# A recurrent mixer's chunk stage: undecayed keys kept and summed for the bonus, end decays straight from PSUM, a later copy, second buffers, another order of pieces

## The chip, the cores and the metric

The kernel runs on one core of one Trainium2 chip. The metric is the device time of one execution in microseconds, the median of several runs. The two layers of the network are written out one after the other in one program, so what one stage gains or loses counts twice.

## The reference, cut to what matters

Each of two layers runs three groups of heads side by side: windowed attention (A), attention with rotary positions (B), and a bidirectional RWKV-7 recurrence (C, six heads of 64). The change touches C alone. Cut to that, for one direction `d`:

```python
decay = exp(-exp(wlog))                                # from tanh(xw) @ w_up[d]
a  = sigmoid(a0[d] + xa @ a_up[d])
kt = heads(k * (1.0 + (a - 1.0) * k_a))                # the undecayed key
for each token:                                        # forward for d = 0, backward for d = 1
    sa = S @ (-kk)
    S  = S * decay + outer(sa, kk * a) + outer(v, kt)
    y  = S @ r
y_sum += y
bonus += sum(r * kt * r_k) * v                         # over both directions
```

The bonus needs, for each token, the sum of `kt` over the two directions.

## The kernel before, in words

C is computed in chunks of 64 tokens. Five tiles of 128 tokens make five groups, each a pair of a forward and a backward tile: (0,3), (1,2), (4,4), (2,1), (3,0). Each tile so comes up twice, once for each direction. For a group g there are four kinds of work:

- `front(g)`: small matmuls give `tanh` of the decay and of `a` (L1074 to L1085), a matmul with a triangle sums the decays (L1092, bank pc), and ACT makes from it the decay `Pe` (L1097) and its inverse `iP` (L1098). `Pe` and `iP` have one buffer each. ACT makes `1 + (a-1) k_a` (L1100), DVE the gradient factor b (L1105, L1113) and the key (L1106, then L1114 with `iP`), POOL and DVE the products `W` (L1111, L1112). POOL copies the end decay PC out of `Pe` (L1117), and ACT copies b into the third part of the tile `BK` (L1115). When a tile comes up the second time, POOL adds `tanh(a)` of that direction into a tile `THS` (L1102). Then PE forms chunk products `GB` (L1130), of which ACT and DVE read the banks (L1132, L1133, L1137), transposes (L1163) follow with ACT copies (L1167).
- `relay(g)`: the 16x16 blocks of a triangular system go through DRAM (L1150, L1174), POOL inverts them on the tile `V` in 15 steps of two operations (L1180, L1182), copies the transpose (L1184), and SP writes both back (L1186). `V` is one tile; the next relay clears it with a memset (L1175).
- `solve(g)`: SP reads the inverses back (L1194), PE widens them to the 64x64 inverse in four rounds (L1202), each ended by a DVE operation (L1213, L1223).
- `step(g, d, i)`: the recurrence over the chunks (L1246 to L1300).

`bonus(t)` forms `z = c2 * THS + c1x2` (ACT, L1337, three times a tile), `z * k` (POOL, L1338), `z * r * r_k` (DVE, L1340) and a matmul.

All of these are generators cut into pieces, and a string of letters, `WEAVE`, says which stream yields its next piece: a, b, g, j, m are front 0 to 4; d, f, i, l, n are solve 0 to 4; e, h, k, o, p are the steps of groups 0 to 4; c builds v and the states; v and w are bonuses and outputs; q to u are out-projection work. "g6" below is the sixth piece of g. The string thus is the order of TensorE (PE); the queues of ACT, DVE, POOL and SP are ordered by a scheduler from the same program. The stage stands at about 303 to 589 us in layer 0 and 1351 to 1633 us in layer 1.

Of the kernel before, what the change touches and what calls it, by code (L numbers as in the profile page):

```python
# [38 lines left out]
WEAVE = ("aqqaaqaqaqqqqqaqqaqqqqaqaqqqqqqqqqcabbabbcbccccdbdccbddcbdccbbbdgdcegddeegggfgfgeegffgefeeeefeeggfjjjhjjhffhjihhhhjhhhjhjhjmmijikiiiimiimmkkmkkmlmkmllkkklkkvlkrlnlnllmnmnnonnnnnrvnonovovvowowvprrroooppwwwssrwpsspssswpwsswppppuwppwstwuxtttttwtttxtyttuuytutxyutuuuuuuuuu",  # L39
         "aqqaaqaqaqqqqqaqqaqqqqaqaqqqqqqqqqcabbabbcbccccdbdccbddcbdccbbbdgdcegddeegggfgfgeegffgefeeeefeeggfjjjhjjhffhjihhhhjhhhjhjhjmmijikiiiimiimmkkmkkmlmkmllkkklkkvlkrlnlnllmnmnnonnnnnrvnonovovvowowvprrroooppwwwssrwpsspssswpwsswppppuwppwstwuxtttttwtttxtyttuuytutxyutuuuuuuuuu")  # L40
# [82 lines left out]
def places(mem):  # L123
# [3 lines left out]
                ("c1x2", 6), ("kkhc", 6), ("sink", 8), ("nsink", 8))  # L127
# [3 lines left out]
    b = mem.lay("F", a, ("THS", 3 * TOK), *many("PC", range(6), 6), ("Pe0", 400), *many("Xf", (0, 1), 384), *many("St", (0, 1), 192), *many("SC", (0, 1), 192))  # L131
# [5 lines left out]
    mem.lay("F", y, ("V", 256), ("iP0", 384))  # L137
# [28 lines left out]
    mem.lay("M", 0, *many("W", (0, 1), 1536), *many("GB", (0, 1), 768), *many("TK", (2, 3), 768), *many("E", (0, 1), 384), *many("Xi", (0, 1), 384))  # L166
# [46 lines left out]
def trunk_kernel(ctx, tc, I, O, dbg=None, depth=DEPTH):  # L213
    nc = tc.nc
# [77 lines left out]
    c1x2 = mem.get("c1x2", [6])  # L292
# [3 lines left out]
    nc.vector.tensor_scalar(out=c1x2, in0=kac, scalar1=-1.0, scalar2=2.0, op0=ALU.mult, op1=ALU.add)  # L296
# [270 lines left out]
    for l in range(depth):  # L567
        if True:
# [499 lines left out]
            def front(g):  # L1068
                for d in range(2):
# [404 lines left out]
            with tc.manual_schedule(engines={PE}):  # L1474
                tiles5 = lambda ts, k0, k1: chain(*[out_part(t, k0, k1) for t in ts])
                streams = [front(0), front(1), chain(calls(*[(build_v, c) for c in range(10)]), calls((states, 0), (states, 1))), solve(0)]
                for g in range(5):
# [3 lines left out]
                    if g < 3:  # L1481
# [162 lines left out]
```

## Time and profile before

| what | before |
|---|---|
| time, median of 3 runs | 2146.09 us (2143.97 to 2146.56) |
| the profiled execution's own time | 2146.71 us |
| its span in the trace | 2144.9 us |
| PE busy | 1957.5 us (91%) |
| DVE, ACT, POOL busy | 1185.5, 815.7, 356.9 us |
| mean granted PE clock | 0.951 |
| the chunk stage of layer 0 | 286 us, PE busy 234.62 us of it |

The own time is the span and 1.8 us around it. PE's share over the whole says that most stages are bound by PE; the chunk stage is where PE has gaps and a lower granted clock, and it is the stage that the change touches.

### The profile page before, as it was taken

To read this page: it belongs to the slowest core of one execution; us is meant where nothing else is said; L and a number is where in the kernel's file an instruction comes from. 1 tells how busy PE (TensorE), PEld (TensorE's weight loads), DVE (VectorE), ACT (ScalarE), POOL (GpSimd) and SP (SyncE) were. 2 spreads that over 40 slices of the span, in tenths; PEclk is the share of its full clock that TensorE was granted. 3 is DMA by queue.
4 is the path that set the end of the run, shared out by engine and by line. 5 is a ranking of instruction groups with operands and counts; after the bars stand their busy time and mean duration, and the time that the engine had idled before them with its cause. 6 is when DMAs were issued, how large, how long until landed. Compare 5 with 4: busy or idle time off the path is not lost. (4 is left out here: it accounts for less than half of the span.)

```text
span 2144.9 us, 40077 instructions
## 1 busy us (share of the span) xinstructions
PE 1957.5 (91%) x16508; PEld 1713.4 (80%) x16508; DVE 1185.5 (55%) x2319; ACT 815.7 (38%) x1787; POOL 356.9 (17%) x644
## 2 busy tenths in 40 slices
PE   7999998778989999999989989968799999999997
PEld 2766787666769979989977878856677998998996
DVE  3657564565876636556267784356677522232324
ACT  4456543342562222212245673343335522221221
POOL 0210012562022112111022000254411000000002
PEclk8999999788999999999999999977899999999999
DMA  8264302224335445354232002022242322222221
GB/s 289 73 204 152 89 24 39 33 44 83 113 103 172 138 128 148 116 150 118 85 101 78 2 2 69 14 45 39 51 125 84 99 79 74 74 74 74 79 69 49
DMA packets 262334, 192.15 MB, mean 90 GB/s; under 512 B 107316, under 2 KB 225038, under 8 KB 262152
## 3 DMA queue, kind: packets, MB, share of 16 engines
q1 hardware_dynamic: 242672, 140.13, 23.6%
q0 software_dynamic: 8800, 29.17, 4.7%
q10 hardware_dynamic: 10680, 20.31, 2.8%
q8 instruction: 129, 2.11, 0.4%
q14 instruction: 53, 0.43, 0.1%
HBM read 173.48 MB, written 16.08 MB: 88 GB/s over the span
## 5 line engine op out<-in xcount | busy, mean ns | idle before, releaser
L549 PE MATMUL psb<-H,B 128*128 128x320 f32 x2112 | 319.8, 311 | 3.6 <-DVE H L541 2.8
L549 PEld LDWEIGHTS psb<-H,B 128*128 128x128 f32 x2112 | 313.5, 189 | 8.5 <-DVE H L541 3.5
L549 PE MATMUL psb<-H,A 128*128 128x320 f32 x2016 | 306.0, 311 | 0.0
L549 PEld LDWEIGHTS psb<-H,A 128*128 128x128 f32 x2016 | 298.4, 189 | 2.2 <-issue 1.2
L367 DVE TENSOR_TENSOR A<-F,A 128x1024 fp32r<-128x1024 f32 (+1 forms) x78 | 93.2, 1195 | 139.2 <-ACT A L366 139.2
L367 DVE TENSOR_TENSOR B<-F,B 128x1024 fp32r<-128x1024 f32 (+1 forms) x78 | 94.1, 1207 | 133.9 <-ACT B L366 133.9
L499 POOL TENSOR_TENSOR r<-v,F 128x1 f32<-128x1 f32 (+1 forms) x50 | 41.1, 824 | 715.6 <-DVE v L497 704.7
L366 ACT CAST A<-F 128x1024 fp32r<-128x1024 f32 (+1 forms) x78 | 80.0, 1026 | 206.8 <-PE psb L549 94.8
L366 ACT CAST B<-F 128x1024 fp32r<-128x1024 f32 x80 | 83.0, 1038 | 180.7 <-PE psb L549 111.1
L549 PE MATMUL psb<-H,C 128*128 128x320 f32 x864 | 130.6, 309 | 0.0
L549 PEld LDWEIGHTS psb<-H,C 128*128 128x128 f32 x864 | 127.8, 188 | 0.2
L400 POOL DMA_DIRECT2D F<-in_w_mod x96 | 71.9, 750 | 326.4 <-DVE F L406 217.5
L408 DVE SCALAR_TENSOR_TENSOR F<-F 128x512 f32<-128x512 f32 x168 | 114.6, 745 | 19.7 <-DMA F<-in_w_mod 14.5
L1572 DVE TENSOR_TENSOR F<-F,psb 128x320 f32<-128x320 f32 x88 | 42.8, 487 | 121.9 <-PE psb L549 121.9
L559 PE MATMUL psb<-A,M 128*128 128x512 f32 x370 | 96.7, 390 | 0.0
L367 DVE TENSOR_TENSOR C<-F,C 128x1024 fp32r<-128x1024 f32 (+1 forms) x34 | 40.5, 1192 | 79.1 <-ACT C L366 79.1
L559 PEld LDWEIGHTS psb<-A,M 128*128 128x128 f32 x370 | 69.2, 188 | 15.4 <-issue 1.0
L559 PE MATMUL psb<-B,M 128*128 128x512 f32 x310 | 77.6, 390 | 0.0
L858 DVE TENSOR_REDUCE mx<-psb 128x1 f32<-128x640 f32 (+3 forms) x100 | 64.6, 648 | 19.6 <-PE psb L840 15.9
L1566 ACT ACTIVATE F<-psb 128x320 f32<-128x320 f32 x88 | 38.2, 435 | 97.2 <-PE psb L549 95.3
L645 PE MATMUL psb<-B,H 128*128 128x512 f32 x240 | 63.6, 410 | 9.0 <-DVE B L367 5.9
L366 ACT CAST C<-F 128x1024 fp32r<-128x1024 f32 (+1 forms) x34 | 34.8, 1022 | 92.1 <-PE psb L559 46.6
(423 smaller groups left out, 3901.4 us busy)
## 6 DMA issues: line engine op xcount, KB each, us to landing
F<-in_w_gu SPq DMA_DIRECT2D x88, 512.0 KB
F<-in_w_mod POOLq DMA_DIRECT2D x96, 256.0 KB, 3.5
F<-in_w_in SPq DMA_DIRECT2D x40, 512.0 KB
F<-in_w_down SPq DMA_DIRECT2D x40, 512.0 KB
F<-in_w_mod SPq DMA_DIRECT2D x26, 512.0 KB
M<-in_w_mod SPq DMA_DIRECT2D x12, 512.0 KB
H<-in_w_mod SPq DMA_DIRECT2D x10, 512.0 KB
F<-in_w_out SPq DMA_DIRECT2D x40, 128.0 KB
```

The costliest lines, as they stand in the source:

```text
L366: nc.scalar.copy(out=hi[:, :n], in_=rawt[:, :n])
L367: (eng or nc.vector).tensor_tensor(out=lo[:, :n], in0=rawt[:, :n], in1=hi[:, :n], op=ALU.subtract)
L400: dma.dma_start(out=rv, in_=w[:, :, c0:c0 + n])
L408: nc.vector.scalar_tensor_tensor(out=ac[s][:, cc], in0=r[:, cc], scalar=sT[:, k, s:s + 1], in1=ac[s][:, cc], op0=ALU.mult, op1=ALU.add)
L499: nc.gpsimd.tensor_tensor(out=r, in0=v, in1=mhalf.to_broadcast(shape), op=ALU.pow)
L549: nc.tensor.matmul(out=ps2[hf][:, :HALF], lhsT=w[:, k, :], rhs=a[k][:, tk], start=(k == 0 and q == 0), stop=(k == KD - 1 and q == 2))
L559: nc.tensor.matmul(out=ps5[t], lhsT=a[k][:, tk], rhs=w[:, kk, :], start=(first and kk == 0 and q == 0), stop=(last and kk == nk - 1 and q ...
L645: nc.tensor.matmul(out=ps, lhsT=a[k0 + kk][:, tk], rhs=w[:, kk, :], start=(i == 0 and q == 0), stop=(i == n - 1 and q == 2))
L858: nc.vector.reduce_max(out=mx, in_=self.S, axis=AX.XY if self.nb == 5 else AX.X)
L1566: nc.scalar.activation(out=sgt[:, HALF * hf:HALF * hf + HALF], in_=pg[hf][:, :HALF], func=AF.Silu)
L1572: nc.vector.tensor_tensor(out=sgt[:, tk], in0=sgt[:, tk], in1=pu[hf][:, :HALF], op=ALU.mult)
```

## The change

- The tile `THS` gives way to `KS`. At a tile's first visit the undecayed key is made in `KS`; at its second in the third part of `BK`, and DVE adds it into `KS`. The POOL addition at L1102 is gone (5 a layer), and so are the bonus's three ACT operations (15 a layer) and its POOL product (5 a layer); five DVE additions a layer are new.
- The end decays PC are made by ACT with an exponential of 128x6 straight from the bank pc (10 a layer) instead of copied by POOL from `Pe`.
- The ACT copy of b moves from the end of the front's second and fourth piece to behind the two `GB` pieces.
- `V` and `iP` get a second buffer each. `Pe` stays at one.
- `WEAVE` is another string of the same letters.

```diff
-WEAVE = ("aqqaaqaqaqqqqqaqqaqqqqaqaqqqqqqqqqcabbabbcbccccdbdccbddcbdccbbbdgdcegddeegggfgfgeegffgefeeeefeeggfjjjhjjhffhjihhhhjhhhjhjhjmmijikiiiimiimmkkmkkmlmkmllkkklkkvlkrlnlnllmnmnnonnnnnrvn...
+WEAVE = ("aqqaaqaqaqqqqqaqqaqqqqaqaqqqqqqqqqcabcabbbdbccccbdcccbdbcdcbbdddgdgdfcebgeegggfgeegffgefeeefeeegjgjhjfjjhffhhjhhhjhhhijhjhjmmijkimiiiiimikmkkmkmlmkmllkkkkllvkklrnlllnmnnmnonnnnnrvn...
...
-            iPR = mem.ring("iP", 1, [3, 2, 64])
+            iPR = mem.ring("iP", 2, [3, 2, 64])
...
-            U, V = (mem.get(nm, [16, 16], parts=96) for nm in ("U", "V"))
+            U, VR = mem.get("U", [16, 16], parts=96), mem.ring("V", 2, [16, 16], parts=96)
...
-                    tha = BK[:, :, :, 2] if t in seen else ch(THS[:, :, tk])
+                    tha = BK[:, :, :, 2]
...
                     nc.scalar.activation(out=iP, in_=pcv[:, :, :, i0:i0 + 64], func=AF.Exp, scale=CDEC)
+                    PC = un["PC"] = PCS.take()
+                    jc = 64 if d == 0 else 0
+                    nc.scalar.activation(out=PC, in_=pcv[:, :, :, jc:jc + 1], func=AF.Exp, scale=-CDEC)
+                    first, KSt = t not in seen, ch(KS[:, :, tk])
+                    kin = KSt if first else BK[:, :, :, 1]
                     for pr in range(3):
-                        nc.scalar.activation(out=BK[:, pr, :, 1], in_=tha[:, pr], func=AF.Identity, scale=col1(c2, pr), bias=col1(c1, pr))
-                    if t in seen:
-                        nc.gpsimd.tensor_tensor(out=ch(THS[:, :, tk]), in0=ch(THS[:, :, tk]), in1=tha, op=ALU.add)
+                        nc.scalar.activation(out=kin[:, pr], in_=tha[:, pr], func=AF.Identity, scale=col1(c2, pr), bias=col1(c1, pr))
...
-                    nc.vector.tensor_tensor(out=BK[:, :, :, 1], in0=BK[:, :, :, 1], in1=ch(ckT[:, :, tk]), op=ALU.mult)
+                    kd = KSt if first else BK[:, :, :, 2]
+                    nc.vector.tensor_tensor(out=kd, in0=kin, in1=ch(ckT[:, :, tk]), op=ALU.mult)
...
-                    nc.vector.tensor_tensor(out=BK[:, :, :, 1], in0=BK[:, :, :, 1], in1=iP, op=ALU.mult)
-                    nc.scalar.copy(out=BK[:, :, :, 2], in_=BK[:, :, :, 0])
-                    jc = 64 if d == 0 else 0
-                    nc.gpsimd.tensor_copy(out=PC, in_=Pe[:, :, :, jc:jc + 1])
+                    nc.vector.tensor_tensor(out=BK[:, :, :, 1], in0=kd, in1=iP, op=ALU.mult)
+                    if not first:
+                        nc.vector.tensor_tensor(out=KSt, in0=KSt, in1=kd, op=ALU.add)
...
                         yield
+                    nc.scalar.copy(out=BK[:, :, :, 2], in_=BK[:, :, :, 0])
                     src = GB
...
-                z = THS[:, :, tk]
-                for pr in range(3):
-                    nc.scalar.activation(out=z[:, pr], in_=z[:, pr], func=AF.Identity, scale=col1(c2, pr), bias=col1(c1x2, pr))
-                nc.gpsimd.tensor_tensor(out=z, in0=z, in1=ckT[:, :, tk], op=ALU.mult)
+                z = KS[:, :, tk]
```

Three places of the queues. First ACT around the second half of front 2 in layer 0, before: L1079 to L1098 make tanh, `Pe` and `iP`; L1337 is the first bonus; L1132 reads the `GB` banks of g5 and g6.

```order
L1079 ACTIVATE F<-psb 128x384
L1085 ACTIVATE F<-psb,F 128x2x64 x3
L1100 ACTIVATE F<-F 128x2x64
L1097 ACTIVATE F<-psb 128x390
L1098 ACTIVATE F<-psb 128x384
L1100 ACTIVATE F<-F 128x2x64 x2
L1337 ACTIVATE F<-F 128x128 x2
L1115 COPY F<-F 128x6x64
L1132 COPY A<-psb 128x3x64
L1337 ACTIVATE F<-F 128x128
L1132 COPY A<-psb 128x3x64
```

The same place after the change (L1078, L1084, L1096, L1097, L1105 and L1134 are L1079, L1085, L1097, L1098, L1100 and L1132 of before; L1100 is the new exponential, L1141 the copy of b):

```order
L1078 ACTIVATE F<-psb 128x384
L1084 ACTIVATE F<-psb,F 128x2x64 x3
L1255 COPY H<-psb 128x192
L1105 ACTIVATE F<-F 128x2x64
L1262 COPY H<-psb 64x192
L1105 ACTIVATE F<-F 128x2x64
L1096 ACTIVATE F<-psb 128x390
L1097 ACTIVATE M<-psb 128x384
L1100 ACTIVATE F<-psb 128x6
L1105 ACTIVATE F<-F 128x2x64
L1134 COPY A<-psb 128x3x64
L1141 COPY F<-F 128x6x64
```

The bonus's L1337 no longer stands ahead of the copies L1134 that empty the `GB` banks; the copy of b stands behind the first of them.

POOL at the end of relay 1 in layer 0, before: L1184 is the relay's last operation, L1175 and L1176 clear `V` for relay 2, L1111 are the `W` products of front 2.

```order
L1184 COPY N<-F 96x256
L1175 MEMSET F 96x256
L1176 MEMSET F 96x16
L1102 TENSOR_TENSOR F<-F 128x3x128
L1111 TENSOR_TENSOR A<-F 64x6x64 x2
L1117 COPY F<-F 128x6
L1338 TENSOR_TENSOR F<-F 128x3x128
L1287 TENSOR_TENSOR F<-H,F 128x192 x3
```

After it (L1188 and L1179 are L1184 and L1175 of before, L1114 is L1111; relay 1 now works on the buffer in zone M):

```order
L1186 TENSOR_TENSOR M<-M,N 96x15
L1188 COPY N<-M 96x256
L1179 MEMSET M 96x256
L1180 MEMSET M 96x16
L1114 TENSOR_TENSOR A<-F 64x6x64 x2
L1291 TENSOR_TENSOR F<-H,F 128x192 x3
```

The additions and the copy are gone, and the memset still stands between the relay's end and the second pair of `W` products, now on the tile that the relay has just left.

DVE around the first rounds of solve 2 (L1213, L1223) and front 4 in layer 0, before; L1340 is the bonus:

```order
L1112 TENSOR_TENSOR H<-C,F 64x6x64
L1113 SCALAR_TENSOR_TENSOR F<-F 128x6x64
L1114 TENSOR_TENSOR F<-F 128x6x64
L1213 TENSOR_TENSOR M<-psb,F 128x384
L1340 SCALAR_TENSOR_TENSOR F<-F 128x128 x3
L1223 TENSOR_TENSOR F<-psb,N 128x384 x2
L1223 TENSOR_TENSOR M<-psb,N 128x384 x2
```

After it (L1217 and L1227 are L1213 and L1223, L1119 is the new addition, L1341 the bonus, L1079 the first DVE operation of front 4's second half):

```order
L1117 TENSOR_TENSOR F<-F 128x6x64
L1119 TENSOR_TENSOR F<-F 128x3x128
L1217 TENSOR_TENSOR M<-psb,F 128x384
L1341 SCALAR_TENSOR_TENSOR F<-F 128x128 x2
L1079 TENSOR_SCALAR F<-F 128x384
L1341 SCALAR_TENSOR_TENSOR F<-F 128x128
L1227 TENSOR_TENSOR F<-psb,N 128x384
```

The bonus's three operations still stand ahead of the second round's L1227, but they need no POOL product any more, and an addition stands ahead of L1217.

## Rows read from the trace of the kernel before

**Rows 1.** The page, engines: busy us, share of the span, instructions.

```profile
PE 1957.5 (91%) x16508; PEld 1713.4 (80%) x16508; DVE 1185.5 (55%) x2319; ACT 815.7 (38%) x1787; POOL 356.9 (17%) x644
```

**Rows 2.** Windows over the stage: length, busy of each engine, PEclk, DMA share, GB/s.

```profile
371.30:403.30 32.00, 18.09 (x272) 14.40 (x272) 14.77 (x31) 13.18 (x35) 17.81 (x41) 0.79 0.30 45
...
458.20:478.80 20.60, 15.97 (x251) 13.64 (x251) 10.78 (x20) 9.14 (x26) 15.34 (x38) 0.75 0.14 19
...
526.80:589.00 62.20, 59.41 (x628) 48.87 (x628) 51.25 (x72) 29.39 (x55) 2.36 (x4) 0.97 0.36 110
sum 286.00, PE 234.62 PEld 200.12 DVE 176.31 ACT 110.94 POOL 98.24; mean PE 23.46 PEld 20.01 DVE 17.63 ACT 11.09 POOL 9.82
```

**Rows 3.** Waits of PE, layer 0: us in total, times, longest.

```profile
PE psb L1130 <- DVE A L1133: 8.4, 1, 8.4
PE psb L1130 <- ACT F L1098: 4.6, 4, 1.7
...
PE psb L1130 <- ACT F L1085: 3.0, 1, 3.0
PE psb L1202 <- DVE F L1223: 2.6, 1, 2.6
...
PE psb L1130 <- POOL H L1111: 1.7, 1, 1.7
PE psb L1202 <- DVE M L1213: 1.5, 1, 1.5
PE psb L1264 <- DVE B L1259: 1.4, 1, 1.4
```

**Rows 4.** Waits of PE, layer 1.

```profile
PE psb L1130 <- DVE A L1133: 8.0, 1, 8.0
```

**Rows 5.** Timeline at g6, SP, POOL, ACT: start, us, what, idle before and releaser.

```profile
371.81 1.25 SPq L1150 DMA_DIRECT2D dN<-F  x2
...
388.68 0.52 POOL L1117 COPY F<-F 128x6 f32<-128x6 f32 x1
...
396.39 0.31 POOL L1175 MEMSET F<- 96x256 f32 x1 [2.03 <-DMA dV<-F]
...
396.94 0.99 POOL L1102 TENSOR_TENSOR F<-F 128x384 f32<-128x384 f32 x1
...
397.96 0.88 ACT L1337 ACTIVATE F<-F 128x128 f32<-128x128 f32 x2 [6.67 <-POOL F L1102]
```

**Rows 6.** Timeline at g6 and f2, PE.

```profile
399.90 2.00 PE L1130 MATMUL psb<-A,F 64*64 64x128 f32 x24 [8.44 <-DVE A L1133]
...
403.26 1.23 PE L1202 MATMUL psb<-N,H 64*64 64x64 f32 x18 [0.69 <-DMA N<-dW]
```

**Rows 7.** One line's instructions, layer 0: ns min/median/max, first and last start.

```profile
L1112 DVE TENSOR_TENSOR H<-C,F x8: 550/581/1197, 346.3 to 480.8; 64x384 f32<-64x384 f32 x8
L1106 DVE TENSOR_TENSOR F<-F x10: 545/558/1255, 305.8 to 479.3; 128x384 f32<-128x384 f32 x10
```

**Rows 8.** Timeline at b4 to b6, ACT, DVE, PE.

```profile
355.62 0.50 ACT L1097 ACTIVATE F<-psb 128x390 f32<-128x390 f32 x1 [3.74 <-POOL F L1117]
356.02 0.48 ACT L1098 ACTIVATE F<-psb 128x384 f32<-128x384 f32 x1
...
360.38 0.32 ACT L1132 COPY H<-psb 128x192 f32<-128x192 f32 x1
...
361.14 0.43 PE L1130 MATMUL psb<-H,F 64*64 64x128 f32 x2 [0.68 <-DVE H L1133]
362.30 0.95 PE L1130 MATMUL psb<-H,F 64*64 64x128 f32 x19 [0.73 <-DVE H L1137]
```

**Rows 9.** Timeline at j4 and j5, ACT.

```profile
432.58 0.51 ACT L1115 COPY F<-F 128x384 f32<-128x384 f32 x1 [3.68 <-POOL F L1102]
...
434.88 0.50 ACT L1097 ACTIVATE F<-psb 128x390 f32<-128x390 f32 x1 [0.66 <-POOL F L1117]
```

**Rows 10.** Timeline at i5 and i6, DVE.

```profile
468.77 1.09 DVE L1340 SCALAR_TENSOR_TENSOR F<-F 128x128 f32<-128x128 f32 x3 [1.99 <-POOL F L1338]
```

More of the change, by code (lines that the diff above doesn't have):

```diff
@@ L38 @@
 TS = (0, 1, 2, 3, 4), (0, 1, 2, 3, 4)
-WEAVE = ("aqqaaqaqaqqqqqaqqaqqqqaqaqqqqqqqqqcabbabbcbccccdbdccbddcbdccbbbdgdcegddeegggfgfgeegffgefeeeefeeggfjjjhjjhffhjihhhhjhhhjhjhjmmijikiiiimiimmkkmkkmlmkmllkkklkkvlkrlnlnllmnmnnonnnnnrvnonovovvowowvprrroooppwwwssrwpsspssswpwsswppppuwppwstwuxtttttwtttxtyttuuytutxyutuuuuuuuuu",
-         "aqqaaqaqaqqqqqaqqaqqqqaqaqqqqqqqqqcabbabbcbccccdbdccbddcbdccbbbdgdcegddeegggfgfgeegffgefeeeefeeggfjjjhjjhffhjihhhhjhhhjhjhjmmijikiiiimiimmkkmkkmlmkmllkkklkkvlkrlnlnllmnmnnonnnnnrvnonovovvowowvprrroooppwwwssrwpsspssswpwsswppppuwppwstwuxtttttwtttxtyttuuytutxyutuuuuuuuuu")
+WEAVE = ("aqqaaqaqaqqqqqaqqaqqqqaqaqqqqqqqqqcabcabbbdbccccbdcccbdbcdcbbdddgdgdfcebgeegggfgeegffgefeeefeeegjgjhjfjjhffhhjhhhjhhhijhjhjmmijkimiiiiimikmkkmkmlmkmllkkkkllvkklrnlllnmnnmnonnnnnrvnoonovrvowrrovwvpooowwpwpsswsprpswssswspswppppuuppwwttsuwuxtttttwtxtyttyttyutxtuuuuuuuuuu",
+         "aqqaaqaqaqqqqqaqqaqqqqaqaqqqqqqqqqcabcabbbdbccccbdcccbdbcdcbbdddgdgdfcebgeegggfgeegffgefeeefeeegjgjhjfjjhffhhjhhhjhhhijhjhjmmijkimiiiiimikmkkmkmlmkmllkkkkllvkklrnlllnmnnmnonnnnnrvnoonovrvowrrovwvpooowwpwpsswsprpswssswspswppppuuppwwttsuwuxtttttwtxtyttyttyutxtuuuuuuuuuu")
 C_ID, C_TRI, C_MK, C_MO, C_MEAN, C_CEN, C_CS, C_AM = 0, 128, 388, 644, 772, 900, 1028, 1284
@@ L126, in places @@
     o = mem.lay("F", 0, ("ct", C_CS), ("mhalf", 1), ("eps12", 1), ("epsgn", 1), ("cols", 128), ("sT", 256), ("sel", 64), ("a0h", 12), ("c1", 6), ("c2", 6),
-                ("c1x2", 6), ("kkhc", 6), ("sink", 8), ("nsink", 8))
+                ("kkhc", 6), ("sink", 8), ("nsink", 8))
     a = mem.lay("F", o, ("oA", 2 * TOK), ("oB", 3 * TOK), ("rT", 3 * TOK), ("bon", 3 * TOK), ("ckT", 3 * TOK), ("sg", TOK))
     mem.lay("F", mem.at["rT"][1], ("qB", 6 * TOK), ("qA", 4 * TOK))
-    b = mem.lay("F", a, ("THS", 3 * TOK), *many("PC", range(6), 6), ("Pe0", 400), *many("Xf", (0, 1), 384), *many("St", (0, 1), 192), *many("SC", (0, 1), 192))
+    b = mem.lay("F", a, ("KS", 3 * TOK), *many("PC", range(6), 6), ("Pe0", 400), *many("Xf", (0, 1), 384), *many("St", (0, 1), 192), *many("SC", (0, 1), 192))
     c = mem.lay("F", b, ("tw", TOK), ("xa", TOK))
@@ L136, in places @@
     y = mem.lay("F", x, ("aup", 768), ("wup", 768))
-    mem.lay("F", y, ("V", 256), ("iP0", 384))
+    mem.lay("F", y, ("V0", 256), ("iP0", 384), ("Pe1", 400))
     w = mem.lay("F", a, ("kA", 1536), ("vA", 768), ("vB", 768))
@@ L165, in places @@
     mem.lay("M", 0, *many("mp", (0, 1), 1024), *many("mp", range(12, 18), 1024))
-    mem.lay("M", 0, *many("W", (0, 1), 1536), *many("GB", (0, 1), 768), *many("TK", (2, 3), 768), *many("E", (0, 1), 384), *many("Xi", (0, 1), 384))
+    mem.lay("M", 0, *many("W", (0, 1), 1536), *many("GB", (0, 1), 768), *many("TK", (2, 3), 768), *many("E", (0, 1), 384), *many("Xi", (0, 1), 384),
+            ("V1", 256), ("iP1", 384))
     mem.lay("N", 0, ("rp0", 1024), ("qk0", 512))
@@ L291, in trunk_kernel @@
     c2 = mem.get("c2", [6])
-    c1x2 = mem.get("c1x2", [6])
     kac = cols[:, col["ka"][0]:col["ka"][0] + 6]
@@ L295, in trunk_kernel @@
     nc.vector.tensor_scalar(out=c2, in0=kac, scalar1=0.5, scalar2=None, op0=ALU.mult)
-    nc.vector.tensor_scalar(out=c1x2, in0=kac, scalar1=-1.0, scalar2=2.0, op0=ALU.mult, op1=ALU.add)
     kkhc = mem.get("kkhc", [6])
@@ L997, in col1 @@
                 return t[:, 3 * l + i:3 * l + i + 1]
-            THS = mem.get("THS", [3, TOK])
+            KS = mem.get("KS", [3, TOK])
             wup, aup = mem.get("wup", [2, 384], parts=65), mem.get("aup", [2, 384])
@@ L1105, in front @@
                     nc.vector.scalar_tensor_tensor(out=BK[:, :, :, 0], in0=tha, scalar=1.0, in1=ch(kkh[:, :, tk]), op0=ALU.add, op1=ALU.mult)
-                    nc.vector.tensor_tensor(out=BK[:, :, :, 1], in0=BK[:, :, :, 1], in1=ch(ckT[:, :, tk]), op=ALU.mult)
+                    kd = KSt if first else BK[:, :, :, 2]
+                    nc.vector.tensor_tensor(out=kd, in0=kin, in1=ch(ckT[:, :, tk]), op=ALU.mult)
                     un["Wn"], W = WS["v"].popleft()
                     un["W"] = W
-                    PC = un["PC"] = PCS.take()
                     for e in range(2):
@@ L1172, in relay @@
             def relay(g):
+                V = VR()
                 nc.sync.dma_start(out=U, in_=diag_blocks(dN[g]))
@@ L1429, in tail_memory @@
             def tail_memory():
-                mem.drop("iP0", "wup", "aup", "th0", "BK0", "BK1", "kkh", "tw", "xa")
+                mem.drop("iP0", "iP1", "wup", "aup", "th0", "BK0", "BK1", "kkh", "tw", "xa")
                 for q in (WS["v"], GBS["v"]):
@@ L1443, in tail_memory @@
                     yield
-                mem.drop("U", "V", "tp", "VD", "WD", "XV1", "XV2", "XV4")
+                mem.drop("U", "V0", "V1", "tp", "VD", "WD", "XV1", "XV2", "XV4")
                 close_w("E", "Xi")
@@ L1488, in trunk_kernel @@
             mem.drop(*[x for x in list(mem.live) if x.rstrip("0123456789") in
-                       ("gup", "dv", "fq", "rs", "THS", "Pe", "PC", "W", "GB", "TK", "Xf", "XV", "ysum", "R", "Ss", "St", "SC", "oA", "oB", "rT", "ckT", "bon", "sg")])
+                       ("gup", "dv", "fq", "rs", "KS", "Pe", "PC", "W", "GB", "TK", "Xf", "XV", "ysum", "R", "Ss", "St", "SC", "oA", "oB", "rT", "ckT", "bon", "sg")])
             hg = open_h()
```

## The prediction

> **What bounds the kernel now.** I read the page first: PE is busy 91% of the span [rows 1], so time can only come out of places where PE waits or runs at a lower clock. The windows over the chunk stage show such a place: PE is busy 234.62 of 286 us [rows 2]. The stage is not even. Its last 62 us are full (59.41 busy), the stretch from 371.3 to 403.3 has 18.09 busy of 32, and the one from 458.2 to 478.8 has 15.97 busy of 20.6 at a granted clock of 0.75 of the full 2.4 GHz, so that PE there ran about half of the time at 1.2 GHz [rows 2]. Third, the waits of PE name the releasers: one wait of 8.4 us at L1130 for a DVE operation, a number of waits of 1 to 3 us at L1130 and at L1202 [rows 3]. Layer 1 shows nearly the same (8.0 for the large one [rows 4]), so I work out one layer and double it. Last I followed each wait in the timeline to what its releaser had itself waited for [rows 5, 6, 8 to 10]; the reader is to see that many of them end at operations that the change moves or removes.
>
> **The largest wait, and why I count almost nothing for it.** At g6 PE sits idle 8.44 us until 399.90 [rows 6]. The timeline explains it backwards: the DVE operation waits for the ACT copy L1132 of the bank, and that stands in ACT's queue behind L1337 of the bonus, which waited 6.67 us for POOL's L1102 at 396.94; POOL came to that only after the memset L1175 of V, which waited 2.03 us for relay 1's DMA to leave V [rows 5]. The change takes L1337 and L1102 out, so this wait should go. But the next piece of the string is f2 (L1202), which needs relay 1's result, and PE waits for that DMA even now, 0.69 us ending at 403.26 [rows 6]. The relay's chain runs from the write of the blocks at 371.81 over POOL's inversion [rows 5] to 403.26 [rows 6]: 31.5 us. None of the edits shortens it but one: POOL's L1117 of 0.52 us lies inside the inversion [rows 5] and leaves POOL. So g6 is done early and PE waits at f2 instead. **B: -0.5.**
>
> **The other edits, per layer.**
>
> A, b4 to b6. `Pe` at 355.62 waited 3.74 us, to its end for POOL's copy L1117, since that reads the one `Pe` buffer; PE's b5 then waits 1.7 for L1111 and up to 1.7 for L1098, and b6 waits 0.68 and 0.73 [rows 3, 8]. Without the copy, `Pe` waits for the product L1111 just ahead of it: about half of a copy of 0.52 [rows 5], 0.25. The ACT copy of b, 0.51 a piece [rows 9], no longer stands ahead of ACT's L1132 at 360.38 [rows 8]: 0.5. The new string sets d1, a solve piece, ahead of b5 instead of behind it; I let it cover a third of b5's second wait, 0.55. **A: -1.3**; bounds 0 and the sum of the four waits, -4.8.
>
> C, j4 and j5. ACT's copy of b, L1115, waited 3.68 us for POOL's L1102 and held L1085 behind it, and PE waits 3.0 us for L1085 [rows 3, 9]. Without both that wait goes, but PE then meets the next one: `Pe` at 434.88 waits for POOL again [rows 9], where L1102 (0.99 [rows 5]) and L1117 leave the queue ahead of it and the products L1111 stay. Those two are up to 1.5 us; some of it comes back as a wait for the products. **C: -1.1**; bounds 0 and -3.0.
>
> D, h6. PE waits 1.4 us for DVE L1259 [rows 3]. The new string puts a piece of j into the run of four h pieces. Half: **D: -0.7**; bounds 0 and -1.4.
>
> E, i5 and i6. PE waits 1.5 for L1213 and 2.6 for L1223 [rows 3]. Ahead of L1223 in DVE's queue the bonus's L1340 waited 1.99 us for POOL's product L1338 [rows 10], which is gone; and the string now sets m3 between i3 and i4, so that PE has other work while DVE does a round. I count both waits as gone, 4.1. The clock of 0.75 over 20.6 us [rows 2] is a loss of 5.15 us; a fuller PE may win back part, and I take about a sixth, 0.9. **E: -5.0**; bounds 0 (the waits go to the next operation on DVE) and -6.7 (half of the clock's loss as well).
>
> F, the five additions on DVE. No row has this very operation. The nearest, L1106, has two SBUF inputs and the same 128x384: 0.545 at least, 0.558 in the middle, 1.255 at most [rows 7]. The additions stand behind the key's product with `iP`, so `GB` doesn't wait for them; what stands behind them on DVE does, L1213 of i5 in one place. Against that the five L1102 no longer run on POOL beside DVE. Bounds: -1 and, with all five on the path at 1.2 us, +6.0. I take **0**, since PE waits for DVE in few of these places. The long times have a cause: L1112, also with two SBUF inputs, is spread from 550 to 1197 ns [rows 7], beside a POOL that does its products at the same times.
>
> The Trainium skill (SBUF — State Buffer, "Who interferes with whom") says that a DVE instruction with two SBUF inputs and a GpSimd instruction that reads SBUF share a read interface, so that the second one waits until the first is done. It speaks against moving a sum from POOL to DVE while POOL's products run, and the spread of L1112 above agrees with it. By the rule alone each addition would be paid at its contended time, and the sum would be 6.0 higher a layer.
>
> G, the exponentials of 128x6 on ACT. ACT took 0.48 us for 128x384 and 0.32 for a copy of 128x192 [rows 8]; 0.16 for 192 columns leaves 0.17 for none, and 0.32 is the upper end. I take 0.25, near the lower end since six columns are almost none: ten of them are 2.5 us of ACT, against fifteen L1337 at 0.44 [rows 5], 6.6 us, that leave. Each holds the pc bank and what is behind it 0.25 longer; in two of ten places something waits. **G: +0.5**; bounds 0 and ten times 0.32, +3.2.
>
> The second buffers of V and iP I count at nothing. POOL's memset still stands directly behind the last copy of a relay, now on the buffer that the relay has just left, and `Pe` has one buffer as before, so `iP` was not what ACT waited for [rows 8]. Were the memset free of the DMA, 2.03 us [rows 5] of POOL would come out, at a place where PE waits for the relay anyway.
>
> Sum of a layer: -0.5 - 1.3 - 1.1 - 0.7 - 5.0 + 0 + 0.5 = -8.1; two layers, -16.2. Against the profiled execution's own 2146.71 us that is 2130.5; this execution lies 0.6 above the median of the three runs, so the prediction is **2130 us**.
>
> **The rivals.** *The large wait goes altogether.* If the waits for relay 1 at f2 were not the next limit, because b9 and the write of the blocks come earlier than I think, or the DMAs come faster, 8.4 and 8.0 us would come out on top: 2130.5 - 16.4 = 2114. For it: the wait at f2 is only 0.69 us now. Against it: that is so because PE arrived late; the chain of 31.5 us is untouched.
>
> *The waits at i5 and i6 are put off, not removed.* DVE still has three L1340 and four rounds of the solve to do in turn, and one addition more ahead of L1213. If E gives nothing, a layer gains 3.1 and the time is 2140.5. For it: solve rounds depend on each other, and an earlier start of one only lets PE meet the next; the low clock before and behind shows that PE lacks work there.
>
> *DVE becomes the bound* (the other side). All five additions of a layer fall on the path at the contended 1.2 us, +6.0, and with DVE full E gives nothing: -8.1 + 6.0 + 5.0 = +2.9 a layer, 2146.71 + 5.8 = 2152.5. It decides from 0.62 us an addition (3.1 over five), given that E gives nothing. For it: contended operations of 1.2 us exist. Against it: POOL has 20 operations fewer beside DVE in a layer, and DVE is busy 176.31 of 286 us [rows 2].
>
> *Nothing is gained.* Each wait that goes reappears at the next piece, since `Pe`, the relay and the solve still run in the same order: 2146.
>
> **How the numbers follow.** Chances: my forecast 0.60 (its own range 2122 to 2137), the large wait altogether gone 0.07, E nothing 0.17, DVE the bound 0.09, nothing gained 0.07. The bound of what a measurement tells from no change is 0.2%, 4.3 us: 2141.8 to 2150.4. Faster: 0.60, 0.07 and 0.13 of the 0.17 (2140.5 lies near the border) make 0.80; same: 0.04 and 0.07, 0.11; slower 0.09. The range runs from the case of 2114 to just above the one of 2140.5, to 2143, where the upper bound of G or a longer wait at f2 would lead it; DVE as the bound, most of "nothing gained" and some of the edges lie outside, about 0.2.
>
> **What the profile after would show.** B: no wait of 8 us at the GB product of g6, and one of some 6 to 8 us for the DMA into N at f2. A and C: waits for `Pe`'s exponential shorter, none for the tanh of j4. E: no waits over 1 us in i5 and i6, and a granted clock above 0.8 there. F: additions at 0.55 to 1.2 us on DVE with no PE wait behind them. The prediction would be wrong if the wait at f2 were longer than the one removed, if the i and m pieces ran at the same clock with the same waits, or if the exponential of 128x6 held the front up.

## The result and the profile after

The changed kernel takes 2122.53 us (median of 4 runs, 2121.1 to 2128.12); the kernel before took 2145.95 in the same comparison. The ratio is 0.9892, with a 95% interval of 0.9876 to 0.9908: 23 us faster, 7 more than the forecast, and inside the range that was given. The page of the changed kernel, the span, the engines (busy us, share, instructions) and the granted clock in 40 slices:

```profile
span 2119.6 us, 40070 instructions
...
PE 1946.4 (92%) x16508; PEld 1707.7 (81%) x16508; DVE 1187.7 (56%) x2328; ACT 805.9 (38%) x1777; POOL 332.4 (16%) x604
...
PEclk8999999789999999999999999988999999999998
```

The span is 25.3 us shorter. POOL lost 24.5 us of work and DVE gained 2.2. PE's instructions are the same and its busy time is 11 us shorter, since it ran less at the lower clock (mean granted clock 0.951 before, 0.958 after). So 11 of the 25 us are PE's own time, and 14 are waits. The windows of the chunk stage of layer 0, cut at the ends of pieces (length, busy of each engine, PEclk, DMA share, GB/s):

```profile
366.60:399.10 32.50, 21.48 (x317) 17.78 (x318) 17.40 (x33) 12.34 (x34) 14.49 (x37) 0.78 0.29 44
...
406.10:432.30 26.20, 19.18 (x320) 16.08 (x320) 15.50 (x32) 11.76 (x34) 16.24 (x40) 0.81 0.16 21
432.30:449.10 16.80, 15.58 (x372) 13.71 (x372) 14.19 (x33) 5.33 (x16) 3.37 (x5) 0.88 0.30 61
449.10:465.10 16.00, 13.64 (x261) 11.43 (x260) 13.36 (x29) 9.12 (x27) 10.54 (x26) 1.00 0.17 33
465.10:482.00 16.90, 10.61 (x222) 8.95 (x224) 9.73 (x23) 3.08 (x12) 6.18 (x15) 0.80 0.61 103
```

The stretch from 449.1 to 465.1 holds i2 to i9 and the first pieces of m, and the next one the rest of m. The same two stretches in the kernel before:

```profile
457.40:479.70 22.30, 16.91 (x257) 14.46 (x258) 12.39 (x23) 10.39 (x28) 16.36 (x40) 0.77 0.18 24
479.70:496.60 16.90, 12.52 (x222) 10.24 (x224) 12.07 (x26) 4.21 (x13) 4.85 (x8) 0.70 0.49 103
```

The first went from a granted clock of 0.77 to 1.00, that is to 2.4 GHz throughout, and PE's busy time for the same matmuls from 16.91 to 13.64 us. The second still has only 10.61 us of PE work in 16.90.

The waits of PE in layer 0 (us in total, times, longest), to be set beside [rows 3]:

```profile
PE psb L1058 <- DMA F<-in_state_c: 5.2, 2, 4.1
PE psb L1260 <- ACT H L1255: 5.1, 1, 5.1
PE psb L1132 <- ACT F L1100: 3.7, 3, 1.5
PE psb L1132 <- DVE A L1135: 3.6, 1, 3.6
PE psb L1132 <- POOL M L1114: 3.0, 1, 3.0
...
PE psb L1206 <- DMA N<-dW: 2.2, 2, 1.4
...
PE psb L1206 <- DVE F L1227: 0.8, 1, 0.8
```

The 8.4 us at g6 are 3.6, the 2.6 at i6 are 0.8, and L1217 (L1213 of before) is gone from the list. The loads of `state_c` cost 5.2 us at c12, where the list of before has 1.4 for them, and new are 5.1 us at L1260, in the piece k4.

To compare the kernels I cut the stage at the last matmul of b9, f2, j5, j10, i9 with m4, m9, o2 and of the out-projection, each taken from the trace together with the pieces that the two strings put on the same side of the cut, and took the differences. (The piece o2 is of solve 4: o is solve 4 and n the steps of group 3, which the list of streams ahead of the prediction has the other way round. The q pieces are the matmuls L964 ahead of b.) Each row is one profiled execution. Us in layer 0 / layer 1:

| kernel | to b9 | to f2 | to j5 | to j10 | to i9, m4 | to m9 | to o2 | to the end | whole stage |
|---|---|---|---|---|---|---|---|---|---|
| before | 30.0 / 29.4 | 33.4 / 32.3 | 32.7 / 32.7 | 20.0 / 20.2 | 22.3 / 22.3 | 16.9 / 16.9 | 30.2 / 28.1 | 62.2 / 60.3 | 286.0 / 281.9 |
| changed | 27.1 / 27.4 | 32.5 / 32.5 | 33.2 / 32.7 | 16.9 / 16.9 | 15.9 / 15.9 | 17.0 / 17.2 | 31.5 / 28.6 | 61.0 / 59.4 | 273.3 / 270.1 |
| new order alone | 28.8 / 29.8 | 34.3 / 34.6 | 32.9 / 33.1 | 21.2 / 20.1 | 20.0 / 20.6 | 20.0 / 16.9 | 31.5 / 28.2 | 60.9 / 59.4 | 287.7 / 282.5 |
| edits, old order | 28.5 / 29.6 | 33.7 / 32.6 | 31.9 / 32.0 | 17.8 / 17.5 | 16.2 / 16.2 | 15.5 / 15.9 | 32.1 / 29.4 | 62.0 / 60.0 | 275.9 / 272.6 |
| keys only, old order | 29.1 / 29.2 | 33.6 / 32.5 | 33.0 / 32.2 | 16.9 / 17.0 | 16.3 / 17.5 | 18.0 / 17.2 | 30.4 / 28.0 | 61.5 / 60.0 | 277.0 / 273.0 |
| sum on POOL | 26.9 / 27.4 | 32.8 / 32.8 | 35.3 / 36.4 | 17.2 / 17.1 | 24.5 / 24.5 | 11.7 / 12.3 | 30.7 / 28.6 | 60.7 / 60.6 | 278.0 / 279.1 |
| one buffer for V and iP | 27.1 / 28.0 | 32.6 / 32.9 | 31.4 / 31.0 | 18.0 / 17.0 | 15.9 / 15.9 | 20.1 / 20.3 | 29.3 / 28.9 | 59.4 / 61.7 | 272.0 / 275.1 |
| end decays on POOL | 28.2 / 29.7 | 33.8 / 33.1 | 33.2 / 33.5 | 16.9 / 16.5 | 16.1 / 16.0 | 17.2 / 16.7 | 32.8 / 29.0 | 60.7 / 60.5 | 277.0 / 274.4 |
| two buffers for Pe | 29.1 / 28.7 | 34.3 / 33.0 | 31.7 / 30.8 | 16.9 / 17.2 | 15.9 / 15.9 | 17.2 / 16.5 | 32.8 / 27.7 | 60.9 / 59.4 | 276.9 / 268.6 |
| residual loads from POOL | 27.1 / 27.7 | 32.3 / 32.4 | 33.5 / 32.7 | 16.6 / 16.3 | 15.9 / 15.9 | 11.7 / 11.7 | 34.4 / 32.6 | 58.0 / 58.2 | 267.8 / 267.0 |
| all products but front 0's on DVE | 26.1 / 26.3 | 31.1 / 31.5 | 28.8 / 30.1 | 17.9 / 17.6 | 15.6 / 15.7 | 13.6 / 13.5 | 32.8 / 30.1 | 58.0 / 58.1 | 262.0 / 262.3 |

The q pieces ahead of b take the same in all. The stage lost 12.7 and 11.9 us, together 24.6 of the 25.3.

Summed over these stretches, from b on, PE's idle time fell from 49.9 and 45.6 us to 41.9 and 41.2, and its busy time, for the same matmuls, from 199.1 and 197.8 to 194.6 and 190.8. In the mean of the layers that is 6.2 us of waits and 5.8 us of PE's own time at a higher granted clock. The split is an account and not two causes: with the keys alone the same sums are 48.7 and 45.6 idle and 191.2 and 189.1 busy.

### The profile page after: what moved, and what is told of

Same layout as the page of the kernel before. It is cut to its first block, busy times and chain, and to the rows that moved or that the text cites. A ratio compares the mean times of both kernels' runs of the same rounds, so it can differ in the third digit from the quotient of the medians.

```text
span 2119.6 us, 40070 instructions
## 1 busy us (share of the span) xinstructions
PE 1946.4 (92%) x16508; PEld 1707.7 (81%) x16508; DVE 1187.7 (56%) x2328; ACT 805.9 (38%) x1777; POOL 332.4 (16%) x604
## 5 line engine op out<-in xcount | busy, mean ns | idle before, releaser
L407 DVE SCALAR_TENSOR_TENSOR F<-F 128x512 f32<-128x512 f32 x168 | 114.6, 747 | 20.1 <-DMA F<-in_w_mod 14.9
```

Source lines behind the costliest of these rows:

```text
L407: nc.vector.scalar_tensor_tensor(out=ac[s][:, cc], in0=r[:, cc], scalar=sT[:, k, s:s + 1], in1=ac[s][:, cc], op0=ALU.mult, op1=ALU.add)
```

## The experiments

Each kernel has its own ratio to the kernel before, from runs on the same chip; the median of before lay between 2140.27 and 2145.95 in these, so the ratios are to be compared rather than the times.

| kernel | median us | ratio | 95% interval |
|---|---|---|---|
| changed | 2122.53 | 0.9892 | 0.9876 to 0.9908 |
| new order alone | 2150.92 | 1.0034 | 1.0020 to 1.0048 |
| edits, old order | 2121.68 | 0.9895 | 0.9874 to 0.9916 |
| one buffer for V and iP | 2124.58 | 0.9919 | 0.9901 to 0.9937 |
| sum on POOL | 2138.91 | 0.9979 | 0.9967 to 0.9991 |
| sum on POOL, key in its own tile | 2138.21 | 0.9972 | 0.9959 to 0.9985 |
| end decays on POOL | 2127.91 | 0.9929 | 0.9915 to 0.9943 |
| copy of b early | 2122.35 | 0.9902 | 0.9887 to 0.9917 |
| keys only, old order | 2128.69 | 0.9935 | 0.9922 to 0.9948 |
| two buffers for Pe | 2125.89 | 0.9927 | 0.9910 to 0.9945 |
| residual loads from POOL | 2111.97 | 0.9863 | 0.9846 to 0.9880 |
| and products of fronts 2 to 4 on DVE | 2107.58 | 0.9827 | 0.9811 to 0.9843 |
| and of front 1 as well | 2100.95 | 0.9797 | 0.9782 to 0.9812 |

**The order or the edits.** The kernel before with the new string:

```diff
-WEAVE = ("aqqaaqaqaqqqqqaqqaqqqqaqaqqqqqqqqqcabbabbcbccccdbdccbddcbdccbbbdgdc...
+WEAVE = ("aqqaaqaqaqqqqqaqqaqqqqaqaqqqqqqqqqcabcabbbdbccccbdcccbdbcdcbbdddgdg...
```

> The kernel before with the new string alone; THS, the POOL sums and copies, the bonus's ACT and POOL work and the single buffers stay. If the edits and the order each give a part (mine): the order fills i5 and i6 with m3, but the 8 us wait at g6 stays, since L1337 still stands behind POOL's sum: 2132 to 2141. If the order does nearly all: 2122 to 2127. If the order only works with the edits: 2145 or more.

And the changed kernel with the string of before, the same diff read the other way:

> The changed kernel with the string of before. If the edits and the order each give a part (mine): the g6 wait moves to f2 for the relay's DMA, i6 no longer waits for POOL's product, so 3 to 5 us a layer: 2134 to 2141. If the edits do nearly all: 2122 to 2127. If the waits that the edits remove all reappear at the next piece: 2145 or more.

The order alone is 0.34% slower; the edits alone give 0.9895, all that the changed kernel has. My reading, a part to each, was wrong: on top of the edits the new string gives nothing that the intervals of about 0.2% tell from zero. In the two profiled executions it is 2.6 and 2.5 us a layer, but the one in the old order was the slowest of its four (2125.61 us). The table shows that the string moves time about: with the edits the stretch to b9 is 1.4 and 2.2 us shorter, that to j5 1.3 and 0.7 longer and that to m9 1.5 and 1.3 longer. The trace of the edits in the old order shows the step that I had worked out for that order. The timeline of PE at g6 and f2:

```profile
393.15 2.00 PE L1132 MATMUL psb<-A,F 64*64 64x128 f32 x24 [3.24 <-DVE A L1135]
...
400.26 0.47 PE L1206 MATMUL psb<-N,H 64*64 64x64 f32 x2 [5.11 <-DMA N<-dW]
401.24 1.23 PE L1206 MATMUL psb<-N,H 64*64 64x64 f32 x18 [0.51 <-DMA N<-dW]
```

The wait at g6 has shrunk from 8.44 [rows 6] to 3.24 us and 5.62 us now stand at f2, for relay 1.

**One buffer for V and iP.** In the changed kernel:

```diff
-            iPR = mem.ring("iP", 2, [3, 2, 64])
+            iPR = mem.ring("iP", 1, [3, 2, 64])
...
-            U, VR = mem.get("U", [16, 16], parts=96), mem.ring("V", 2, [16, 16], parts=96)
+            U, VR = mem.get("U", [16, 16], parts=96), mem.ring("V", 1, [16, 16], parts=96)
```

> The changed kernel with one buffer for V and one for iP again. Counted at nothing (mine): within 2 us of the changed kernel, 2121 to 2125. If the second buffers carry a part of the gain (ACT's exponential for iP waits for the last reader on DVE, the relay's memset for the DMA that reads V): 2127 or more.

The intervals of this kernel and of the changed one overlap, and the medians are 2.05 us apart, at the edge of what I had set. The stretch to m9 is 3 us longer and that to j5 1.7 shorter. Whether the second buffers give something stays open; it is 0.3% at most by the middle values.

**The additions on DVE or on POOL.** In the changed kernel:

```diff
-                        nc.vector.tensor_tensor(out=KSt, in0=KSt, in1=kd, op=ALU.add)
+                        nc.gpsimd.tensor_tensor(out=KSt, in0=KSt, in1=kd, op=ALU.add)
```

> The changed kernel with the five KS additions a layer on POOL instead of DVE. If the additions on DVE cost nothing on the path (mine): 2121 to 2127, no gain from taking them off DVE, perhaps a loss since on POOL they stand behind the relays and the copy of b waits for them. If they are on the path at a contended 0.55 to 1.2 us: faster by 3 to 8 us, 2114 to 2119.

Neither held: the kernel loses 0.87%, most of the gain. My first guess was that ACT stands behind POOL at the copy of b, which overwrites the key and so waits for the sum. So, on top of this edit, the second visit's key got a tile of its own, K2, in the place laid for a second `Pe` buffer:

```diff
+            K2 = mem.get("Pe1", [400])[:, 0:384].rearrange("p (q c j) -> p q c j", q=3, c=2)
...
-                    kd = KSt if first else BK[:, :, :, 2]
+                    kd = KSt if first else K2
```

> The changed kernel with the KS additions on POOL, and the second visit's key in a tile of its own, so that ACT's copy of b does not wait for the addition. If the loss of the addition on POOL (2138.9) came from ACT standing behind POOL and the relay at that copy (mine now): back to 2121 to 2127. If it came from POOL's own time, ahead of the products W and inside the relays: stays at 2132 to 2140.

That fell too: 2138.21 is no better and lies in the range of the other reading. The timeline of this kernel shows what it is (POOL, DVE and PE; L1120 is the sum, L1342 the bonus, L1228 and L1207 the solve):

```profile
474.12 0.60 POOL L1189 COPY N<-M 96x256 f32<-96x256 f32 x1
474.68 0.99 POOL L1120 TENSOR_TENSOR F<-F 128x384 f32<-128x384 f32 x1
...
475.70 1.00 DVE L1342 SCALAR_TENSOR_TENSOR F<-F 128x128 f32<-128x128 f32 x1 [8.09 <-POOL F L1120]
476.62 0.54 DVE L1228 TENSOR_TENSOR M<-psb,N 128x384 f32<-128x384 f32 x1
...
477.22 1.55 PE L1207 MATMUL psb<-M 64*64 64x64 f32 x24 [7.77 <-DVE M L1228]
```

The sum of a tile stands on POOL behind the whole of relay 3; DVE comes to the bonus of that tile, waits 8.09 us for the sum, and the solve's next operation, which has its data, stands behind it. PE waits 7.77 us. So at this place it is POOL's queue, not POOL's speed: 0.99 us of work there costs DVE 8. The table shows the same in the stretch to i9 and m4, which is 24.5 us with the sum on POOL and 15.6 to 17.5 in the kernels that have it on DVE. Of these 8.6 us the next stretch gives 5 back (11.7 and 12.3 us), since the wait at k4, told below, is spent meanwhile. The stretch to j5 loses 2.1 and 3.7 more in the same way: behind relay 2 DVE's bonus waits 7.07 us for a sum (428.28 us), and PE at j4 4.39 us for the DVE operation behind it.

**The keys alone.** The kernel before with the keys kept and summed on DVE; the string, the single buffers, POOL's copy of the end decays and the early copy of b as they were:

```diff
+                    first, KSt = t not in seen, ch(KS[:, :, tk])
...
+                        nc.vector.tensor_tensor(out=KSt, in0=KSt, in1=kd, op=ALU.add)
...
-                    nc.scalar.activation(out=z[:, pr], in_=z[:, pr], func=AF.Identity, scale=col1(c2, pr), bias=col1(c1x2, pr))
-                nc.gpsimd.tensor_tensor(out=z, in0=z, in1=ckT[:, :, tk], op=ALU.mult)
```

> The kernel before with the keys kept and summed on DVE alone: old string, single buffers, end decays copied on POOL, copy of b at the old place. If the gain is the bonus and sum leaving POOL and ACT (mine now): 2121 to 2129. If the gain needs the other three edits as well: 2132 to 2141.

0.9935, at the upper end of the range that I had set: this edit is worth 0.65%, 14 of the 23 us, and the stretches to j10 and to i9, m4 have nearly their full gain from it, in the old order.

**The end decays and the copy of b.** The changed kernel with the end decays on POOL:

```diff
-                    nc.scalar.activation(out=PC, in_=pcv[:, :, :, jc:jc + 1], func=AF.Exp, scale=-CDEC)
...
+                    nc.gpsimd.tensor_copy(out=PC, in_=Pe[:, :, :, jc:jc + 1])
```

> The changed kernel with the end decays copied on POOL from Pe again. If the exponential on ACT takes POOL's copy out of relay 1 and off the wait of the next Pe (mine, terms A and B less G): 1 to 4 us slower, 2123 to 2127. If the ten exponentials only hold the bank and ACT: no slower, 2119 to 2122.

It loses 0.37%, 8 us by the ratios (5.4 by the medians), more than the 4 that I had set as the most. The stretch to b9 is 1.1 and 2.2 us longer, that to f2 1.3 and 0.6. ACT at b4 to b6 of this kernel in layer 0:

```profile
353.27 0.50 ACT L1096 ACTIVATE F<-psb 128x390 f32<-128x390 f32 x1 [2.28 <-POOL F L1117]
...
356.84 1.28 ACTq L1053 DMA_DIRECT2D F<-in_state_c  x2
358.15 0.32 ACT L1134 COPY H<-psb 128x192 f32<-128x192 f32 x1 [3.61 <-PE psb L1045]
```

In the changed kernel `Pe` starts at 353.02, so POOL's copy delays it by only 0.25 us. The larger part is behind it. ACT also issues the state loads, which go into the `Pe` buffer, and the second copy on POOL (356.40 to 356.80) still reads that buffer. So the issue stands until 356.84, and the copy L1134 that empties the `GB` bank of b5 comes at 358.15 instead of 356.78; PE waits 0.97 us more at b6.

And the copy of b at its old place:

```diff
                     if not first:
                         nc.vector.tensor_tensor(out=KSt, in0=KSt, in1=kd, op=ALU.add)
+                    nc.scalar.copy(out=BK[:, :, :, 2], in_=BK[:, :, :, 0])
                     yield
...
-                    nc.scalar.copy(out=BK[:, :, :, 2], in_=BK[:, :, :, 0])
```

> The changed kernel with ACT's copy of b at the end of the front's piece, behind the sum (the tile part is the key's until then), as before. If its place ahead of the copies that empty the GB banks costs PE (mine, 0.5 a piece at b6 and part of C): 2 to 6 us slower, 2124 to 2129. If what held ACT was only POOL's sum, which is gone either way: 2120 to 2123.

2122.35, no difference that the intervals show: what had held ACT at this copy [rows 9] was POOL's sum.

**What bounds the stretches that did not shorten.** Two buffers for `Pe`, in the changed kernel:

```diff
-            PeR = mem.ring("Pe", 1, [400])
+            PeR = mem.ring("Pe", 2, [400])
```

> The changed kernel with two buffers for Pe (its place is laid already). If the waits of ACT's exponential for POOL's products, and of c12's state loads, which use the Pe ring, are what PE now waits for at c12 and j5 (5.2 and 4.5 us in layer 0): 3 to 8 us faster than the changed kernel, 2114 to 2120. If relay 1 sets the time of f2 and the products behind relay 2 that of j5 anyway, as I argued of the g6 wait: within 2 us, 2120 to 2125.

No gain: 0.9927 is a loss of 0.35%, with an interval that does not meet that of the changed kernel. The wait at c12 is gone, that at g6 is 2.57 us, and the time is at f2 (timeline of PE):

```profile
401.97 0.47 PE L1206 MATMUL psb<-N,H 64*64 64x64 f32 x2 [10.03 <-DMA N<-dW]
```

So relay 1 does set the time of f2 here. In the changed kernel other waits just cover its chain, by this estimate: here f2 starts 3.8 us after the issue of the relay's last load (398.19 to 401.97), there 4.6 us after it (392.56 to 397.19), with no wait at f2.

**The new wait at k4.** The changed kernel's rows there, POOL, ACT's queue, ACT and PE:

```profile
469.41 1.92 POOL L1114 TENSOR_TENSOR H<-F 64x384 f32<-64x384 f32 x2
...
471.36 0.36 ACTq L1502 DMA_DIRECT2D F<-in_x_prompt  x1
471.77 0.32 ACT L1255 COPY H<-psb 128x192 f32<-128x192 f32 x1 [6.51 <-POOL H L1114]
...
472.14 0.91 PE L1260 MATMUL psb<-H,F 64*64 64x64 f32 x12 [5.07 <-ACT H L1255]
```

ACT issues the load of a residual tile, which waits for the last products on POOL, behind relay 3; ACT's copy for k4 is queued behind the issue. So the loads were given to another queue:

```diff
-                nc.scalar.dma_start(out=x2[t], in_=src)
+                nc.gpsimd.dma_start(out=x2[t], in_=src)
```

> The changed kernel with the reload of the residual tiles issued from POOL instead of ACT. In the changed kernel that issue waits in ACT's queue for POOL's last products and holds the copy L1255, for which PE waits 5.1 us at k4. If that wait is the length of the m pieces: 2 to 4 us a layer, 2114 to 2119. If the products that POOL makes behind relay 3 set the same moment: no change, 2120 to 2125. If the loads come late or hold POOL: slower.

2111.97, 0.9863, though this interval still meets that of the changed kernel (0.9876 to 0.9880). The stretch to m9 is 11.7 us in both layers instead of 17.0 and 17.2, and its granted clock 1.00 instead of 0.80. Some of it comes back, as the stretch to o2 is 34.4 and 32.6, 3 to 4 longer: there PE now waits 2.43 and 1.28 us for relay 3's data (layer 0).

**POOL's products on DVE.** On top of the last, `W` products:

```diff
-                        nc.gpsimd.tensor_tensor(out=W[HS[e], e, :, :, 64:128], ...
+                        (nc.vector if g >= 2 else nc.gpsimd).tensor_tensor(out=W[HS[e], e, :, :, 64:128], ...
```

> The kernel of the last run (residual loads issued from POOL) with the W products of fronts 2, 3 and 4 on DVE instead of POOL, six tiles a layer, two products each. If PE at g6 and j5 waits because these products stand on POOL behind the relays and slow DVE beside them (mine): the j5 stretch loses 2 to 4 us a layer, f2 stays with relay 1, 2103 to 2109. If twelve more operations of 0.55 us a layer make DVE the bound, the rival of my prediction: 2114 or more.

and with `g >= 1`:

> As the run before, with front 1's products on DVE as well. If DVE has room there too: b4 to b9 shorter by up to 2 us a layer, 2100 to 2108. If DVE is the bound in b5 to b9, where it already reads the GB banks: 2 to 4 us longer than the run before.

0.9827 and 0.9797, both in the ranges that I had set. The stretch to j5 goes from 33.5 and 32.7 to 30.1 and 29.2, the one to f2 from 32.3 and 32.4 to 31.5 and 30.8, and with front 1 the one to b9 from 27.1 and 28.0 to 26.1 and 26.3. The instructions of the products in the last kernel (ns min/median/max, first and last start):

```profile
L1114 DVE TENSOR_TENSOR H<-F x8: 540/559/876, 347.0 to 459.8; 64x384 f32<-64x384 f32 x8
...
L1114 POOL TENSOR_TENSOR M<-F x4: 1119/1208/1297, 305.2 to 311.9; 64x384 f32<-64x384 f32 x4
```

0.559 us on DVE against 1.208 on POOL. The neighbours of the moved products on DVE (L1115 on tiles H and A) are no longer slowed: they took 543 to 654 ns, against up to 1180 in the changed kernel. This is the fastest kernel of the study, 45 us ahead of the kernel before.

## Why the prediction was right, and where its steps were not

The layers gained 12.7 and 11.9 us where the sum said 8.1. The sum was made of waits, 7.2 us, and of 0.9 us for the clock, in E alone. The trace has 6.2 us less waiting and 5.8 us less of PE's own time. So the waits were about right in total and the clock was the term put far too low. By the terms, as means over the two layers from the table:

- **A and B**, b4 to b6 and relay 1: -1.3 and -0.5 were forecast; the stretches to b9 and f2 lost 2.5 and 0.4. B was right in mechanism and size: relay 1 sets f2, as the kernels with the old order and with two `Pe` buffers show. The profile after did not show the 6 to 8 us at f2 that I had named, since the new order and the state loads put the same idle time to c12 (5.2) and g6 (4.2). A was mis-sized. `Pe` is 0.25 us later with POOL's copy, as forecast, but the sum left out that the same copy holds the state loads, whose issue stands in ACT's queue ahead of b6. Taking the copy back costs 1.1 and 2.2 us to b9. The part for the order, 0.55, rests on a misreading: d1 only issues loads and has no matmul, so it can't cover a wait of PE. The stretch is 1.4 and 2.2 shorter with the new order all the same, for a reason that I haven't traced. The part for the copy of b is nothing.
- **C**, j5: -1.1 was forecast, and the stretch is 0.2 longer. What the term was about did come. From the end of relay 2's last copy to the end of j5 it took 5.8 us before (431.60 to 437.37) and 4.4 after (427.85 to 432.27). But relay 2 itself ended 2.0 us later behind f2 (26.8 us before, 28.8 after), which the term took as fixed; a write of its blocks took 1.5 us longer, for which SP waits 3.2 us in all against 1.7. With the edits in the old order the stretch is 0.8 and 0.7 shorter than before. The wait that is left is one of 2.99 us for POOL's products, which stand behind relay 2's last copy (L1188, 427.25 to 427.85). With them on DVE the stretch loses 3 us; whether their length or their place in POOL's queue counts was not tried apart.
- **D**, h and j pieces: -0.7 was forecast for a piece of j in the run of h; it is -3.2. The wait of 1.38 us that the term was about is gone in the changed kernel and still 1.3 with the edits in the old order, whose stretch is 0.9 and 0.6 longer, so the piece of j does what I said. But most of the gain is there without it, since the keys alone give it in the old order (16.9 and 17.0). That D came out with the right sign owes much to luck. Of the 3.2 us, 1.8 are PE's own time (17.6 us before, 15.6 and 16.0 after). What went with the keys is the bonus's part on ACT and POOL. That this stretch held POOL's L1338 beside DVE's L1340 is read from the trace before; which of the two engines' relief counts was not tried apart.
- **E**, i5 and i6: -5.0 was forecast, -6.4 is measured. Of it 3.0 us are waits, where 4.1 were forecast, and 3.3 are PE's own time at a clock of 1.00 instead of 0.77, where 0.9 were. I gave the waits to two causes, POOL's product ahead of DVE's L1340 and m3 between i3 and i4. It is the first: the old order has 16.2, and the sum on POOL, in the new order, 24.5. The order alone had 20.0 and 20.6.
- **F**, the additions on DVE at 0: right in size. They took 545 to 590 ns. The sign that I had named, no PE wait behind them, did not hold in one place: the addition at 394.12 stands directly ahead of L1135, for which PE waits 3.58 us at g6, so up to 0.55 us of that wait is the addition. The rival in which DVE becomes the bound is refuted: taking the additions off DVE costs 16 us by the medians, and DVE took another sixteen products a layer with a gain.
- **G**, the exponentials at +0.5: the operation took 0.183 us, at the lower end of the bounds (which by its rows is 0.16, not 0.17). PE's waits end at it in six places, but it ends only 0.07 us behind the `iP` exponential ahead of it (430.66 and 430.59), so 0.4 us is my estimate of its cost. The whole edit is a gain, by the run with POOL's copy.

The lines of the changed kernel for F and G, with POOL's steps of relay 3 beside the addition at 457.63 and the same two steps of relay 1, at 378 us, where no addition runs:

```profile
L1119 DVE TENSOR_TENSOR F<-F x5: 545/558/590, 394.1 to 462.3; 128x384 f32<-128x384 f32 x5
...
L1100 ACT ACTIVATE F<-psb x10: 182/183/193, 305.3 to 465.1; 128x6 f32<-128x6 f32 x10
...
378.08 0.23 POOL L1186 TENSOR_TENSOR M<-M,N 96x28 f32<-96x28 f32 x1
378.39 0.26 POOL L1184 TENSOR_TENSOR N<-M,N 96x39 f32<-96x39 f32 x1
...
457.37 0.43 POOL L1186 TENSOR_TENSOR M<-M,N 96x28 f32<-96x28 f32 x1
457.63 0.59 DVE L1119 TENSOR_TENSOR F<-F 128x384 f32<-128x384 f32 x1
457.88 0.46 POOL L1184 TENSOR_TENSOR N<-M,N 96x39 f32<-96x39 f32 x1
```

By the rule of the Trainium skill (SBUF — State Buffer, "Who interferes with whom") the additions would have been paid at their contended time. It holds where DVE met POOL's products: in the changed kernel DVE's L1116 took 1.28 us at 392.45 beside them, against 0.56 alone. None of the additions met a product. Three of the five ran beside steps of a relay on POOL and took 558 to 590 ns, so hardly longer, while POOL's steps there took 0.43 and 0.46 us instead of 0.23 and 0.26.

Of the rivals, the one in which the waits at i5 and i6 are only put off had a true part: a wait of 5.07 us appeared at k4, in the next stretch, which kept its length, and it was no solve round but an issue of a load in ACT's queue.

## What to carry to other kernels

A short operation in the queue of an engine that also runs a long serial chain (here POOL's relays of some 14 us) costs what its consumers wait for the chain, not its own duration: 0.99 us on POOL held DVE 8.09. So look at where a small operation stands in its queue, and who stands behind its consumer, before asking which engine does it fastest. A wait of many us in front of another chain is worth little: find what the next piece waits for first, and try it by removing the wait alone. And a load's issue is an entry in the issuing engine's queue, which here held what was behind it until the load's place was free: the issue of a residual tile held ACT's copy for k4 6.51 us. Last, when a change takes waits away, look at the granted clock of the stretch before and after: here the clock's part was as large as that of the waits, and the sum had a ninth of its gain for it.

## What the runs showed of the hardware that was not expected

The exponential of 128x6 took 0.183 us on ACT. The Trainium skill (ScalarE: Activation LUTs, "What ACT_TABLE_LOAD costs") gives 186 ns and 0.833 ns for each column where scale and bias are constants, an estimate of 191 ns for six columns; the trace agrees within 8 ns. DVE did a product of 64x384 in 0.559 us in the middle where POOL took 1.208. In the stretch to i9 and m4 the granted clock was 0.77 in both layers of the kernel before, where PE waited 1.5 and 2.6 us, and 1.00 in both layers of the changed one, where its longest wait was 0.8 us. DVE's additions took 558 to 590 ns beside POOL's steps of a relay, and it was POOL's steps that took longer, 0.43 and 0.46 us instead of 0.23 and 0.26.
